# Making the lo parts of six output-projection weight tiles with adding transfers of GpSimd's queue

## The chip, the core and the metric

The kernel runs on one core of one Trainium2 chip. The metric is the device time of one execution in microseconds. The time before is 1053.56 us, the median of 3 runs (1052.34 to 1053.63).

## The reference

One decoder layer for 256 tokens of width 2048, all in float32:

```
h  = rmsnorm(x);  p = h @ w_in            # 16 heads: 8 dilated-window heads, 8 latent heads
A, B = the two attentions of p
x  = x + rmsnorm(concat(A, B) @ w_out)    # w_out: 2048 x 2048  <- the stage of the change
x  = x + rmsnorm(square(relu(rmsnorm(x) @ w_up)) @ w_down)
```

`concat(A, B)` is 256 x 2048 (`mixT`, transposed, in the kernel), so the output projection multiplies 2 blocks of 128 tokens by 16 blocks of 128 weight rows and 4 blocks of 512 weight columns.

## The kernel before

**Three products for one.** TensorE multiplies float32 in its faster form fp32r. To keep the accuracy, each operand is split in two: `hi` is the value rounded to fp32r, `lo` is what is left, `value - hi`. A product is then `hi*hi + lo*hi + hi*lo`, three matmuls that add up in one PSUM bank. The split of a weight tile takes two instructions (lines 293 and 294): ScalarE (ACT) writes `hi` as a rounded copy of the loaded tile `raw`, and VectorE (DVE) writes `lo = raw - hi`.

**Weight tiles.** All weights pass through the class `Weights` in one numbered series of tiles of 128 x 1024 (512 KB). `raw` has 5 buffers, `hi` and `lo` have 8 each. A tile is recorded (load, `hi`, `lo`) 7 tiles ahead of the one that TensorE works on. Loads are issued by SyncE (SP). A load waits until its `raw` buffer has been read for the last time; a split waits for its load and until TensorE has finished the tile that stood in the same `hi` and `lo` buffers, 8 tiles before.

**The output projection.** `ch_o` is four chunks of 512 columns, 0 to 3, each of 8 weight tiles; a tile holds two blocks of 128 rows. TensorE takes chunks 0 and 1 first, together; then chunk 2, tile by tile for both token blocks; then chunk 3, whose tiles 0 to 2 are taken for both token blocks at once and whose tiles 3 to 7 are taken for block 0 first and then for block 1. Tiles carry their number in the series: chunk 2 is tiles 105 to 112 and chunk 3 is tiles 113 to 120, so `hi106` is `hi` of the second tile of chunk 2. Tiles from 121 on are the first of `w_up`. A tile that both token blocks use at once is 12 matmuls.

**What else goes on there.** The last two heads of the latent attention (`b6`, `b7`) end inside chunks 0 and 1; their result `o_b` goes over ACT (`mixT_hi`) and DVE (`mixT_lo`) back to TensorE. When chunk 0 ends, `g_post` (1 MB, the gain of the norm) is loaded by SP into space that the attention has just left. ACT squares each finished chunk out of PSUM (`junko`) and DVE multiplies it by `g_post` (`yg`), which frees the PSUM bank. `powers()` squares `g_post` on ACT in four pieces (`junkg`), sums them on DVE (`gg`, `pws`, `t_pw`), and takes a power on GpSimd (`rstd_pw`), with which DVE scales `x`.

**Order.** Each engine runs its instructions in the order in which the program records them, and waits at the first one that is not ready. `Flow` records the attention and norm steps between the matmuls by an estimated clock of the author's; the weights are recorded by `Weights.emit` at the moment when TensorE's work reaches the tile 7 before.

Of the kernel before, what the change touches and what calls it, by code (L numbers as in the profile page):

```python
# [18 lines left out]
F32 = mybir.dt.float32  # L19
# [3 lines left out]
AF = mybir.ActivationFunctionType  # L23
OP = mybir.AluOpType
PSUM = bass.MemoryType.PSUM

P = 128
# [85 lines left out]
class Flow:  # L113
# [3 lines left out]
    def __init__(self):  # L117
        self.clock = 0.0
        self.chains = []
# [34 lines left out]
class Weights:  # L154


    def __init__(self, nc, pool, split, bufs, ahead):
        self.nc, self.pool, self.split_fn = nc, pool, split
        self.bufs, self.limit, self.ahead = bufs, bufs, ahead
        self.specs, self.tiles, self.done = [], [], []  # L160
        self.first, self.queue = {}, {}

    def plan(self, *spec):

# [13 lines left out]
    def emit(self, upto):  # L178
        upto = min(upto, self.done.index(False) + self.limit, len(self.specs))
        while len(self.tiles) < upto:  # L180
            i = len(self.tiles)
            spec = self.specs[i]
            make = len(spec) == 1
            if make or i not in self.queue:
                for f in self.first.pop(i, ()):
                    f()
            if not make:
                src, nk, n, g = (*spec, None)[:4]
                w = nk * n
                raw = self.load(src if len(src.shape) == 3 else src.rearrange("(k p) n -> p k n", p=P), w, f"raw{i}",  # L190
                                self.queue.get(i))
                for f in self.first.pop(i, ()):
                    f()
            hi = self.pool.tile([P, CW], F32R, tag="hi", bufs=self.bufs, name=f"hi{i}")
            lo = self.pool.tile([P, CW], F32R, tag="lo", bufs=self.bufs, name=f"lo{i}")
            if make:
                spec[0](hi, lo)
                self.tiles.append((hi, lo))
                continue

            def v(t):
                return t[:, :w].rearrange("p (k n) -> p k n", k=nk)

            cuts = [(o, min(o + 512, w)) for o in range(0, w, 512)] if i < FINE else [(0, w)]
            for o, e in cuts:
                self.split_fn(hi[:, o:e], lo[:, o:e], raw[:, o:e], g)
            self.tiles.append((v(hi), v(lo)))
# [43 lines left out]
def layer(nc, tc, io):  # L251
# [49 lines left out]
    def tok(t, k, b):  # L301
        return t[:, k, b * P:(b + 1) * P]

    weights = Weights(nc, wp, split, W_BUFS, W_AHEAD)
    gcol = con.tile([P, 8 + KD], F32, name="gcol")


# [17 lines left out]
    ch_o = [Chunk(weights, io["w_out"], n * 512, 512, K2, plan=False) for n in range(4)]  # L325
    for n, m in ((0, 6), (1, 6), (0, 2), (1, 2), (2, 8), (3, 8)):
        ch_o[n].plan(m)
    def up_weight(j, k):
        return io["w_up"][k * P:(k + 1) * P, j * CW:(j + 1) * CW]

# [32 lines left out]
    def seven_up(j, kp):  # L363
        def load():
            if j == FF // CW - 1 and kp:
                return [weights.load(up_weight(j, 2 * kp + i), CW, f"raw_w{j}_{kp}{i}") for i in range(2)]
            return load_two(late["ab"], nc.gpsimd if (j, kp) > (1, 0) else nc.sync,
                            io["w_up"][2 * kp * P:(2 * kp + 2) * P, j * CW:(j + 1) * CW])

        return seven(load, lambda: [late["up"].tile([P, CW], F32, tag="T", bufs=2, name=f"{n}{j}_{kp}") for n in "tu"])  # L370
# [21 lines left out]
    def plan_seven(sums, fs, after, more=(), last=()):  # L392

        at = max(len(weights.specs) - SUMS_AHEAD, after)
        for n, f in (*more, (0, sums), *((0, f) for f in last)):
            weights.first.setdefault(at - n, []).append(f)
        return [weights.plan(f) for f in fs], len(weights.specs)
# [4 lines left out]
    for j in range(FF // CW):  # L402
        wide_u.append([])
        for what, k in [("k", k) for k in range(KD)] if j == 0 else UP_STEPS:
            if what == "k":
                ts = [weights.plan(up_weight(j, k), 1, CW, gcol[:, 8 + k:9 + k])]
            else:
                ts, after = plan_seven(*seven_up(j, k), after)
            wide_u[j].append((what, k, ts))

    def down_weight(c, k):
        return io["w_down"][k * P:(k + 1) * P, c * CW:(c + 1) * CW]

    def seven_down(c, kp):
        def load():

            n = DOWN_SEVEN[c].index(kp)
            raw = dpl["ab"]
            if n % 2:
                raw = [uT[i].rearrange("p k s -> p (k s)") for i in range(2)] if c else late["c"]  # L420
            return load_two(raw, nc.gpsimd, io["w_down"][2 * kp * P:(2 * kp + 2) * P, c * CW:(c + 1) * CW])

        return seven(load, lambda: [late["st"][:, i * CW:(i + 1) * CW] for i in range(2)])

    dpl, left, skeep, wide_d = {}, {}, {}, []
    for c in range(2):
        wide_d.append([])
        for what, k in DOWN_STEPS[c]:
            if what == "k":
                ts = [weights.plan(down_weight(c, k), 1, CW)]  # L430
            else:
                q, parts_q, back = [lambda c=c, k=k, f=f: f(c, k) for f in (down_sums, down_split, down_back)]
                more = ((), (back,)) if c and k in SHARED else (((2, q), (1, parts_q)),)
                ts, after = plan_seven(*seven_down(c, k), after, *more)
# [218 lines left out]
    for half in range(2):  # L653
        qkv = {}
        for nms in (("qk", "v") if not half else "qkv"):
            accs = [acc for _, _, acc in proj(xT, [ch_a[half, nms]], f"{nms}{half}",
                                              bank_of=at_bank if (half, nms) == (0, "v") else None)]
            for i, nm in enumerate(nms):
                t = pa.tile([P, NB, 512], F32, tag=nm, name=f"{nm}_{half}")
# [215 lines left out]
    for ns in ((0, 1), (2,), (3,)):  # L875
# [4 lines left out]
        for c, b, acc in proj(mixT, [ch_o[n] for n in ns], f"o{ns[0]}", order, heads_done):  # L880
            n = ns[c]
            if not late:
# [8 lines left out]
                                  in_=io["norm_attn_post"].partition_broadcast(P).rearrange("p o d -> p (o d)"))  # L891
# [124 lines left out]
    for j in range(FF // CW):  # L1016
# [9 lines left out]
        for t, b in order:  # L1026
            what, k, tiles = steps[t]
# [172 lines left out]
    for g in (GT - 2, GT - 1):  # L1200
        if g == GT - 1:
            nc.gpsimd.drain()
        for b, n in PARTS:
            for kk in range(4):
                k = 4 * g + kk
# [40 lines left out]
def build(nc, arrays):  # L1246
    io = {n: nc.dram_tensor(f"in_{n}", a.shape, mybir.dt.from_np(a.dtype), kind="ExternalInput").ap()
          for n, a in arrays.items()}
    io["out"] = nc.dram_tensor("out_0", (S, D), F32, kind="ExternalOutput").ap()
    with tile.TileContext(nc) as tc, tc.manual_schedule():  # L1250
        layer(nc, tc, io)
# [12 lines left out]
```

## Time and profile before

| | |
|---|---|
| median of 3 runs | 1053.56 us (1052.34 to 1053.63) |
| the profiled execution's own time | 1052.05 us |
| its span, from the first to the last instruction | 1050.3 us |
| TensorE (PE) busy | 1039.0 us, 99% of the span |
| VectorE (DVE) busy | 811.0 us, 77% |
| ScalarE (ACT) busy | 625.4 us, 60% |
| GpSimd (POOL) busy | 61.5 us, 6% |
| granted TensorE clock | 0.998 |
| chunk 2 of the output projection, by TensorE | 309.7 to 331.5 us |
| chunk 3 | 331.5 to 354 us |

Between the span and the execution's own time lie 1.75 us outside the recorded instructions. The execution is 1.5 us below the median of the runs. In the tables of windows, `PE busy (x)` is the busy time and in brackets the number of instructions. In a timeline a row is: start, duration, engine, line, operation, output <- inputs, and in brackets the idle time before it with what ended it. Rows of DMA issues give the size of one transfer and the median time from issue to landing; POOLq and SPq are the queues of GpSimd and SyncE.

### The profile page before, as it was taken

What the parts mean: (1) busy time and instruction counts of PE and PEld (TensorE: products, weight loads), DVE (VectorE), ACT (ScalarE), POOL (GpSimd) and SP (SyncE); (2) the same over time, 40 slices, a digit from 0 to 9 for tenths busy, and PEclk for the clock granted to TensorE, in tenths of its full rate; (3) what the DMA queues carried; (4) which work ended last, traced back from release to release, by engine and by line L of the source; (5) the groups of instructions that cost most, each with busy time, mean ns of one, the idle gap of its engine ahead of it and who ended that gap; (6) DMA issues with size and microseconds to landing.
All of it is one profiled execution on the core that took longest, in us unless ns stands there. A gap on an engine that the chain in (4) does not pass through costs nothing.

```text
span 1050.3 us, 13459 instructions
## 1 busy us (share of the span) xinstructions
PE 1039.0 (99%) x4854; PEld 865.9 (82%) x4854; DVE 811.0 (77%) x1080; ACT 625.4 (60%) x834; POOL 61.5 (6%) x116
## 2 busy tenths in 40 slices
PE   9999999999999999999999999999999999999996
PEld 6888899888888788888888888888888888888885
DVE  6676536577557679879888798887899978989995
ACT  6675436565555467666665666666567564766661
POOL 0000000000000000010000000000000001112100
PEclk9999999999999999999999999999999999999999
DMA  8975447454447295646556465469788767788952
GB/s 298 371 230 155 140 127 239 141 166 155 141 170 234 77 344 174 224 143 238 194 189 201 145 234 194 151 227 319 246 276 315 267 223 259 268 300 313 381 186 81
DMA packets 80643, 229.34 MB, mean 218 GB/s; under 512 B 7616, under 2 KB 12224, under 8 KB 80192
## 3 DMA queue, kind: packets, MB, share of 16 engines
q1 hardware_dynamic: 65888, 176.45, 50.3%
q0 software_dynamic: 14112, 51.39, 14.2%
q8 instruction: 38, 0.62, 0.2%
q10 hardware_dynamic: 576, 0.64, 0.2%
q14 instruction: 29, 0.24, 0.1%
HBM read 212.72 MB, written 15.73 MB: 218 GB/s over the span
## 4 chain that ended last, share of the span: by engine, by line
PE 96%; DVE 1%; DMA 1%; issue 1%; ACT 0%; POOL 0%; DVEq 0%; POOLq 0%; ACTq 0%
PE y L283 26%; PE acc_u L283 26%; PE acc_o L283 8%; PE m L283 5%; PE md L283 5%; PE acc_v L283 4%; PE acc_qk L283 4%; PE acc_ckv L283 2%; PE acc_ukv L283 2%; PE acc_q L283 2%; PE acc_cq L283 2%; PE acc_k L283 2%; PE acc_uq L283 2%; PE rt L287 1%; PE sc_b L283 1%
## 5 line engine op out<-in xcount | busy, mean ns | idle before, releaser
L294 DVE TENSOR_TENSOR lo<-raw,hi 128x1024 fp32r<-128x1024 f32 (+3 forms) x213 | 241.7, 1152 | 91.5 <-ACT hi L293 90.7
L293 ACT ACTIVATE hi<-raw 128x1024 fp32r<-128x1024 f32 (+3 forms) x213 | 209.5, 999 | 77.6 <-PE y L283 20.8
L283 PE MATMUL acc_u<-hi,hT_hi 128*128 128x512 f32 x386 | 153.3, 397 | 0.0
L283 PE MATMUL acc_u<-hi,hT_lo 128*128 128x512 f32 x386 | 151.0, 391 | 0.4 <-DVE hT_lo L294 0.4
L283 PE MATMUL acc_u<-lo,hT_hi 128*128 128x512 f32 x386 | 150.7, 391 | 0.0
L283 PE MATMUL y<-hi,uhi 128*128 128x512 f32 x376 | 146.8, 390 | 0.0
L283 PE MATMUL y<-hi,ulo 128*128 128x512 f32 x376 | 146.5, 390 | 0.0
L283 PE MATMUL y<-lo,uhi 128*128 128x512 f32 x376 | 146.5, 390 | 0.0
L298 DVE SCALAR_TENSOR_TENSOR lo<-raw,gcol,hi 128x1024 fp32r<-128x1024 f32 x86 | 107.6, 1280 | 11.2 <-ACT hi L297 11.0
L297 ACT ACTIVATE hi<-raw,gcol 128x1024 fp32r<-128x1024 f32 x86 | 97.8, 1151 | 24.8 <-PE acc_u L283 10.9
L283 PEld LDWEIGHTS acc_u<-hi,hT_lo 128*128 128x128 f32 x386 | 72.5, 188 | 16.1 <-DVE hT_lo L294 0.8
L283 PEld LDWEIGHTS acc_u<-lo,hT_hi 128*128 128x128 f32 x386 | 72.6, 188 | 14.2
L283 PEld LDWEIGHTS acc_u<-hi,hT_hi 128*128 128x128 f32 x386 | 72.6, 188 | 13.9
L283 PEld LDWEIGHTS y<-hi,uhi 128*128 128x128 f32 x376 | 70.6, 188 | 14.6
L283 PEld LDWEIGHTS y<-hi,ulo 128*128 128x128 f32 x376 | 70.6, 188 | 14.6
L283 PEld LDWEIGHTS y<-lo,uhi 128*128 128x128 f32 x376 | 70.6, 188 | 14.5
L283 PE MATMUL acc_o<-hi,mixT_hi 128*128 128x512 f32 x128 | 51.9, 405 | 0.0
L294 DVE TENSOR_TENSOR lo<-st_down,hi 128x1024 fp32r<-128x1024 f32 x40 | 48.1, 1220 | 4.0 <-ACT hi L293 3.8
L283 PE MATMUL acc_o<-hi,mixT_lo 128*128 128x512 f32 x128 | 50.2, 392 | 0.0
L283 PE MATMUL acc_o<-lo,mixT_hi 128*128 128x512 f32 x128 | 50.0, 391 | 0.0
L293 ACT ACTIVATE hi<-ab 128x512 fp32r<-128x512 f32 (+1 forms) x38 | 32.0, 842 | 29.3 <-PE acc_u L283 24.4
L293 ACT ACTIVATE hi<-st_down 128x1024 fp32r<-128x1024 f32 x40 | 42.1, 1053 | 11.1 <-PE y L283 9.5
(322 smaller groups left out, 1986.3 us busy)
## 6 DMA issues: line engine op xcount, KB each, us to landing
raw<-in_w_down SPq DMA_DIRECT2D x88, 512.0 KB, 6.0
raw<-in_w_up SPq DMA_DIRECT2D x86, 512.0 KB, 4.5
raw<-in_w_in SPq DMA_DIRECT2D x55, 512.0 KB, 5.0
ab<-in_w_up POOLq DMA_DIRECT2D x36, 512.0 KB, 5.0
raw<-in_w_out SPq DMA_DIRECT2D x32, 512.0 KB, 4.3
ab_down<-in_w_down POOLq DMA_DIRECT2D x20, 512.0 KB, 6.4
ukeep<-ulo SPq DMA_DIRECT2D x15, 512.0 KB, 7.2
ulo<-ukeep POOLq DMA_DIRECT2D x15, 512.0 KB, 5.4
```

The costliest lines, as they stand in the source:

```text
L283: nc.tensor.matmul(out, a, b, start=start, stop=stop)
L287: nc.tensor.transpose(out, a, ident)
L293: nc.scalar.activation(hi, src, AF.Copy)
L294: nc.vector.tensor_tensor(out=lo, in0=src, in1=hi.bitcast(F32), op=OP.subtract)
L297: nc.scalar.activation(hi, src, AF.Copy, scale=g)
L298: nc.vector.scalar_tensor_tensor(out=lo, in0=src, scalar=g, in1=hi.bitcast(F32), op0=OP.mult, op1=OP.subtract)
```

## The change

For six tiles of the output projection `lo` is no longer written by VectorE. ScalarE writes `lo = -hi`, and a transfer issued by GpSimd, with an addition on the way, adds the float32 values to it.

- Tiles 106, 108, 110 and 112 (tiles 1, 3, 5, 7 of chunk 2; "sbuf"): SP loads `raw` as before. ACT writes `hi` (line 319 after the change) and then `lo = -hi` as a second rounded copy of `raw` with scale -1 (line 320). GpSimd issues the transfer `lo += raw` from SBUF to SBUF (line 321).
- Tiles 114 and 117 (tiles 1 and 4 of chunk 3; "hbm"): there is no `raw` and no load by SP. GpSimd loads the tile from HBM straight into `hi`, converted to fp32r on the way (line 315); ACT writes `lo = -hi` (line 316); GpSimd issues `lo += weights` from HBM (line 317), which reads the tile from HBM a second time.

```diff
--- before.py
+++ after.py
@@ -158,7 +158,7 @@
         self.nc, self.pool, self.split_fn = nc, pool, split
         self.bufs, self.limit, self.ahead = bufs, bufs, ahead
         self.specs, self.tiles, self.done = [], [], []
-        self.first, self.queue = {}, {}
+        self.first, self.queue, self.adds = {}, {}, {}
 
     def plan(self, *spec):
 
@@ -184,9 +184,11 @@
             if make or i not in self.queue:
                 for f in self.first.pop(i, ()):
                     f()
+            by = self.adds.get(i)
             if not make:
                 src, nk, n, g = (*spec, None)[:4]
                 w = nk * n
+            if not make and by != "hbm":
                 raw = self.load(src if len(src.shape) == 3 else src.rearrange("(k p) n -> p k n", p=P), w, f"raw{i}",
                                 self.queue.get(i))
                 for f in self.first.pop(i, ()):
@@ -201,6 +203,11 @@
             def v(t):
                 return t[:, :w].rearrange("p (k n) -> p k n", k=nk)
 
+            if by:
+                self.add_fn(hi, lo, src if by == "hbm" else raw, v)
+                self.tiles.append((v(hi), v(lo)))
+                continue
+
             cuts = [(o, min(o + 512, w)) for o in range(0, w, 512)] if i < FINE else [(0, w)]
             for o, e in cuts:
                 self.split_fn(hi[:, o:e], lo[:, o:e], raw[:, o:e], g)
@@ -301,7 +308,20 @@
     def tok(t, k, b):
         return t[:, k, b * P:(b + 1) * P]
 
+    def split_by_add(hi, lo, src, v):
+
+        if len(src.shape) == 2 and src.shape[0] != P:
+            src = src.rearrange("(k p) n -> p k n", p=P)
+            nc.gpsimd.dma_start(out=v(hi), in_=src)
+            nc.scalar.activation(lo, hi.bitcast(F32), AF.Copy, scale=-1.0)
+            nc.gpsimd.dma_start(out=v(lo), in_=src, accum_op=OP.add)
+        else:
+            nc.scalar.activation(hi, src, AF.Copy)
+            nc.scalar.activation(lo, src, AF.Copy, scale=-1.0)
+            nc.gpsimd.dma_start(out=lo.bitcast(F32), in_=src, accum_op=OP.add)
+
     weights = Weights(nc, wp, split, W_BUFS, W_AHEAD)
+    weights.add_fn = split_by_add
     gcol = con.tile([P, 8 + KD], F32, name="gcol")
 
 
@@ -325,6 +345,9 @@
     ch_o = [Chunk(weights, io["w_out"], n * 512, 512, K2, plan=False) for n in range(4)]
     for n, m in ((0, 6), (1, 6), (0, 2), (1, 2), (2, 8), (3, 8)):
         ch_o[n].plan(m)
+    for n, ts, how in ((2, (1, 3, 5, 7), "sbuf"), (3, (1, 4), "hbm")):
+        for t in ts:
+            weights.adds[ch_o[n].tiles[t][0]] = how
     def up_weight(j, k):
         return io["w_up"][k * P:(k + 1) * P, j * CW:(j + 1) * CW]
```

TensorE's order is the same before and after. On VectorE six subtractions are gone, in SyncE's queue the loads `raw114` and `raw117`; the rest keeps its order there. The two engines whose order changes are shown here; in the rows the numbers behind the underscore are buffer numbers.

GpSimd's instructions from the clearing of `krT` (attention) to the first `rstd_post` (the norm after the projection), before:

```order
L710 MEMSET krT_1891 128x512
L485 TENSOR_TENSOR rstd_pw_3002<-t_pw_3001,neg_half_82 128x2
L485 TENSOR_TENSOR rstd_post0_3196<-t_post0_3195,neg_half_82 128x1
L485 TENSOR_TENSOR rstd_post1_3312<-t_post1_3311,neg_half_82 128x1
L485 TENSOR_TENSOR rstd_pre20_3343<-t_pre20_3342,neg_half_82 128x1
```

The same stretch of GpSimd after the change:

```order
L733 MEMSET krT_1891 128x512
L321 DMA lo106_2779<-raw106_2776 128x1024
L321 DMA lo108_2836<-raw108_2833 128x1024
L321 DMA lo110_2898<-raw110_2895 128x1024
L321 DMA lo112_2945<-raw112_2942 128x1024
L315 DMA hi114_2983<-in_w_out 128x2x512
L317 DMA lo114_2984<-in_w_out 128x2x512
L508 TENSOR_TENSOR rstd_pw_3005<-t_pw_3004,neg_half_82 128x2
L315 DMA hi117_3052<-in_w_out 128x2x512
L317 DMA lo117_3053<-in_w_out 128x2x512
L508 TENSOR_TENSOR rstd_post0_3198<-t_post0_3197,neg_half_82 128x1
```

Eight transfers have come in. `rstd_pw` now stands behind six of them, and the load of `hi117` stands behind `rstd_pw`.

ScalarE's instructions from the end of chunks 0 and 1 (`junko`, out of their four PSUM banks) through the splits of chunk 2's last and chunk 3's first tiles, before:

```order
L293 ACTIVATE hi110_2895<-raw110_2893 128x1024
L802 ACTIVATE junko10_2905,ssy0_2433<-acc_o0_1_0_0_2448 128x512
L802 ACTIVATE junko11_2914,ssy1_2434<-acc_o0_1_1_0_2449 128x512
L293 ACTIVATE hi111_2921<-raw111_2919 128x1024
L816 ACTIVATE junkg0_2937,gg4_2437<-g_post_2859 128x512
L293 ACTIVATE hi112_2941<-raw112_2939 128x1024
L816 ACTIVATE junkg1_2954,gg4_2437<-g_post_2859 128x512
L293 ACTIVATE hi113_2961<-raw113_2959 128x1024
L816 ACTIVATE junkg2_2971,gg4_2437<-g_post_2859 128x512
L293 ACTIVATE hi114_2981<-raw114_2979 128x1024
L816 ACTIVATE junkg3_2988,gg4_2437<-g_post_2859 128x512
```

After, from the second copy of tile 112 to the split of tile 118:

```order
L320 ACTIVATE lo112_2945<-raw112_2942 128x1024
L839 ACTIVATE junkg1_2958,gg4_2437<-g_post_2861 128x512
L300 ACTIVATE hi113_2965<-raw113_2963 128x1024
L839 ACTIVATE junkg2_2975,gg4_2437<-g_post_2861 128x512
L316 ACTIVATE lo114_2984<-hi114_2983 128x1024
L839 ACTIVATE junkg3_2991,gg4_2437<-g_post_2861 128x512
L300 ACTIVATE hi115_3010<-raw115_3008 128x1024
L300 ACTIVATE hi116_3035<-raw116_3033 128x1024
L316 ACTIVATE lo117_3053<-hi117_3052 128x1024
L300 ACTIVATE hi118_3072<-raw118_3070 128x1024
```

The copies `lo112` (and, above these rows, `lo106`, `lo108` and `lo110`) are new on ScalarE. `lo114` and `lo117` stand where `hi114` and `hi117` stood, but read what GpSimd's transfers bring. The same kind of insertion stands between the last two steps of head b7: before it was the copy of `hi108` and then `mixT_hi` from `o_b7`, after it is

```order
L320 ACTIVATE lo108_2836<-raw108_2833 128x1024
L300 ACTIVATE mixT_hi_76<-o_b7_2840 128x256
```

with `hi108` ahead of both.

## The prediction

> **What bounds the kernel now.** I read the page's busy times first, then TensorE's waits, then the windows of 8 us over the stage that changes.
>
> ```profile
> span 1050.3 us, 13459 instructions
> PE 1039.0 (99%) x4854; PEld 865.9 (82%) x4854; DVE 811.0 (77%) x1080; ACT 625.4 (60%) x834; POOL 61.5 (6%) x116
> ...
> PE warm L505 <- DVE zero L502: 1.2, 1, 1.2
> PE acc_qk L283 <- ACT hi L293: 1.0, 2, 0.8
> PE acc_u L283 <- DVE hT_lo L294: 0.4, 1, 0.4
> PE qrt L287 <- DVE qT L744: 0.2, 1, 0.2
> ```
>
> TensorE is the bound: 1039.0 of 1050.3 us, and all its recorded waits together are 2.8 us, none of them for a weight tile of the output projection. So taking work off VectorE in this stage has almost nothing to give, and the change can only be felt if a tile that was ready in time comes late. What matters is by how much each of the six tiles was early, and how long its new way is.
>
> ```profile
> 302.00:310.00 8.00, 8.00 (x36) 6.37 (x36) 2.31 (x5) 2.71 (x6) 0.00 (x0) 1.00 0.92 314
> 310.00:318.00 8.00, 8.00 (x37) 6.64 (x36) 6.97 (x8) 7.97 (x16) 0.00 (x0) 1.00 0.97 343
> 318.00:326.00 8.00, 8.00 (x37) 6.64 (x36) 7.23 (x16) 3.40 (x5) 1.60 (x1) 1.00 0.91 281
> 326.00:334.00 8.00, 8.00 (x37) 6.60 (x36) 4.37 (x6) 4.01 (x7) 0.00 (x0) 1.00 0.53 178
> 334.00:342.00 8.00, 8.00 (x37) 6.64 (x36) 5.22 (x5) 3.78 (x4) 0.00 (x0) 1.00 0.71 231
> ```
>
> The columns are the stretch, its length, busy PE, PEld, DVE, ACT and POOL, the granted clock, the DMA share and GB/s. TensorE is never idle at full clock. What is scarce from 302 to 326 is the transfers (shares 0.92, 0.97, 0.91), because the loads held back behind `g_post` are being caught up, and from 310 to 318 ScalarE (7.97 of 8 us). The change adds to exactly these two.
>
> **When TensorE needs the tiles.** The first matmul of chunk 2 is at 309.72, the first that reads `lo114` at 334.42, the first that reads `lo117` at 341.22:
>
> ```profile
> 309.72 0.39 PE L283 MATMUL acc_o<-hi,mixT_hi 128*128 128x512 f32 x1
> ...
> 334.42 0.39 PE L283 MATMUL acc_o<-lo,mixT_hi 128*128 128x512 f32 x1
> ...
> 341.22 0.39 PE L283 MATMUL acc_o<-lo,mixT_hi 128*128 128x512 f32 x1
> ```
>
> They are found by counting rows of TensorE's order, which starts a matmul every 0.2267 us here ((341.22 - 309.72) / 139). By the same count `lo106` is due at 312.67, `lo108` at 318.1, `lo110` at 323.55 and `lo112` at 329.0.
>
> **The change, part by part.** *VectorE loses six subtractions.*
>
> ```profile
> L294 DVE TENSOR_TENSOR lo<-raw,hi 128x1024 fp32r<-128x1024 f32 x14 | 17.1, 1224 | 5.1 <-ACT hi L293 4.9
> ```
>
> That is 6 x 1.224 = 7.3 us of busy time off the path; no tile of the stage was waited for, so it is worth 0. *ScalarE gains four copies* (the "sbuf" tiles; the "hbm" tiles trade one for one), about 1.05 us each. One of them, `lo108`, stands ahead of head b7's `mixT_hi` (timelines of ScalarE, VectorE and TensorE):
>
> ```profile
> 299.86 1.05 ACT L293 ACTIVATE hi<-raw 128x1024 fp32r<-128x1024 f32 x1
> 301.46 0.39 ACT L293 ACTIVATE mixT_hi<-o_b 128x256 fp32r<-128x256 f32 x1 [0.54 <-PE o_b L283]
> ...
> 300.95 1.23 DVE L294 TENSOR_TENSOR lo<-raw,hi 128x1024 fp32r<-128x1024 f32 x1 [0.66 <-ACT hi L293]
> 302.09 0.42 DVE L294 TENSOR_TENSOR mixT_lo<-o_b,mixT_hi 128x256 fp32r<-128x256 f32 x1
> ...
> 302.56 0.50 PE L283 MATMUL acc_o<-hi,mixT_lo 128*128 128x512 f32 x1
> ```
>
> `hi108` ends at 300.91, `lo108` would end near 301.9, so `mixT_hi` starts 0.4 later than 301.46. `mixT_lo` was held to 302.09 by the subtraction of tile 108, which is gone, so it moves only to about 302.4. The matmul at 302.56 started right behind it; 0.3 us of TensorE are lost here, with nothing to hide them (bounds 0 and 0.5).
>
> *The transfers that add.* No row shows one. The nearest:
>
> ```profile
> ab<-in_w_up POOLq DMA_DIRECT2D x36, 512.0 KB, 5.0
> ukeep<-ulo SPq DMA_DIRECT2D x15, 512.0 KB, 7.2
> ulo<-ukeep POOLq DMA_DIRECT2D x15, 512.0 KB, 5.4
> c<-in_w_down POOLq DMA_DIRECT2D x8, 512.0 KB, 8.1
> ...
> L360 POOL DMA_DIRECT2D ab<-in_w_up x36 | 19.6, 544 | 251.3 <-DVE lo L294 223.7 <-DVE c L963 27.7
> ```
>
> At least an add is a plain transfer of GpSimd's queue into such a tile, 5.4 us. At most it is as long as reading the tile out and bringing it back one after the other, 7.2 + 5.4 = 12.6 us. It must fetch two operands for every value written, so I take the middle, 9.0 us; the nearest row is the 8.1. The plain load of `hi` by GpSimd, converting on the way, I take at 5.0 us (the `ab` row; bounds 5.0 and 8.1). Eight issues at 0.54 us are 4.3 us of GpSimd, which was idle.
>
> The Trainium skill ("Collectives: The Full Stack", Part 3, "The bandwidth ceiling") says that an adding transfer costs not by its arithmetic but by its two source reads, and moves at about half the rate of a copy (32.35 against 62.28 GB/s). No row here shows it; it speaks for a price above 5.4.
>
> *The chain of the last tile.* The rows of the timelines of ScalarE, VectorE and GpSimd that it starts from:
>
> ```profile
> 308.39 1.06 ACT L293 ACTIVATE hi<-raw 128x1024 fp32r<-128x1024 f32 x1 [3.17 <-DMA raw<-in_w_out]
> 309.73 1.06 ACT L293 ACTIVATE hi<-raw 128x1024 fp32r<-128x1024 f32 x1 [0.27 <-DMA raw<-in_w_out]
> 310.70 0.57 ACT L802 ACTIVATE junko<-acc_o 128x512 bf16<-128x512 f32 x1
> ...
> 314.49 0.62 ACT L816 ACTIVATE junkg<-g_post 128x512 bf16<-128x512 f32 x1
> ...
> 316.67 1.05 ACT L293 ACTIVATE hi<-raw 128x1024 fp32r<-128x1024 f32 x1
> 317.62 0.62 ACT L816 ACTIVATE junkg<-g_post 128x512 bf16<-128x512 f32 x1
> ...
> 319.34 0.17 DVE L484 TENSOR_SCALAR t_pw<-pws 128x2 f32<-128x2 f32 x1
> ...
> 319.59 1.60 POOL L485 TENSOR_TENSOR rstd_pw<-t_pw,neg_half 128x2 f32<-128x2 f32 x1 [112.66 <-DVE t_pw L484]
> ```
>
> ScalarE waited for the load of tile 109 until 308.39. The add of tile 108, issued near 301.9, now shares the engines with that load. Its 0.52 MB read twice are 1.05 MB; at the 314 GB/s of that window 3.3 us; half of it ahead of tile 109's bytes delays ScalarE by 1.7 us (bounds 0 and 3.3). Then ScalarE runs without a gap as before, with two copies of 0.97 us more (the step from 309.73 to 310.70): `lo112` ends at 314.49 + 1.7 + 2 x 0.97 = 318.1. GpSimd issues the add of 112 there and at 318.7 the load of `hi114` (its buffer, that of tile 106, was left by TensorE near 315). It lands after 5.0 us, and 1.7 us later still for the add just ahead of it in the same queue: 325.4 (bounds 323.7 and 327.2). ScalarE, which stands at `lo114` from 316.67 + 1.7 + 1.94 = 320.3, waits 5.1 us. `lo114` ends at 326.4, its add lands at 335.4; TensorE asks at 334.42 + 0.3 = 334.7 and waits 0.7.
>
> Behind `lo114` is the fourth `junkg`: 0.7 us, then about 0.6 us of `gg`, `pws` and `t_pw` on a VectorE with time: 327.7. `rstd_pw` takes 1.60: 329.3. Only now does GpSimd issue `hi117`; it lands at 334.3, `lo117` is written by 335.35, its add lands 9.0 us later at 344.35. TensorE, late by 0.3, asks at 341.5. So it waits 2.85 us, which includes the 0.7. Sum: 0.3 + 2.85 = 3.1 us.
>
> Rows for what stands around the new steps: VectorE's first product with `g_post`, the issue of `g_post`, SP's loads of the stage, and the first use of the scaled `x`.
>
> ```profile
> L803 DVE TENSOR_TENSOR yg<-acc_o,g_post 128x512 f32<-128x512 f32 x6 | 4.0, 687 | 6.5 <-DMA g_post<-in_norm_attn_post 3.9 <-ACT junko L802 2.5
> ...
> 301.58 0.34 SPq L890 DMA_DIRECT2D g_post<-in_norm_attn_post  x1
> ...
> 306.44 1.29 DVE L803 TENSOR_TENSOR yg<-acc_o,g_post 128x512 f32<-128x512 f32 x2 [3.93 <-DMA g_post<-in_norm_attn_post]
> ...
> raw<-in_w_out SPq DMA_DIRECT2D x12, 512.0 KB, 5.8
> ...
> 349.14 2.08 DVE L841 SCALAR_TENSOR_TENSOR x<-yg,rstd_post,x 128x512 f32<-128x512 f32 x3 [0.66 <-POOL rstd_post L485]
> ```
>
> *What queues behind.* Behind ScalarE's wait for `hi117` stand `hi118` (due 342.4, ready with its subtraction near 337.6), the two `junko` of chunk 2 (their banks are next needed by `acc_u` near 354) and tiles 119 and 120, due 1.4 us apart after 343.7: late by some 6 us against before, still ahead of use. SP's loads 113, 116 and 119 now wait for the adds of 108, 110 and 112, which held their `raw` buffers; 116 is issued near 322 and needed by ScalarE near 328, so with the 5.8 us of landing that SP's loads take in this stage it just fits. `rstd_pw` moves from 319.59 to about 327.7; the scaled `x` that waits for it is first used at 349.14.
>
> **Against which time.** The profiled execution took 1052.05 us (span 1050.3 and 1.75 around it); with 3.1 it becomes 1055.2. The median of the runs was 1053.56, so I forecast 1053.56 + 3.1 = 1056.7 us.
>
> **Rivals.** *Everything stays hidden* (not slower). The case turns on the add's duration: the add of `lo117` starts at 335.35 and is due at 341.5, so up to 6.15 us it costs nothing, and a plain 5.4 is under that. For it: the lower row, and the windows of 326 to 342 with DMA shares of 0.53 and 0.71, where a transfer meets little. Against it: two operands per value. Then only b7's 0.3 us remain: 1053.9. The Trainium skill ("DMA: Bandwidth & Descriptors", "Anatomy of one DMA") gives 2.0 us fixed and bytes at 436 GB/s; with doubled reads that is an estimate of 4.4 us for an add on an empty queue, and the sum by it is this rival's.
>
> *The add of 108 holds up `g_post`* (slower, early). `g_post` landed just before 306.44, `yg` freed chunk 2's first bank at 307.1, TensorE asked at 309.72: 2.6 us of room, 2.9 with b7's 0.3. The add's 3.3 us, all ahead of `g_post`, would cost 0.4; if it takes twice that, 3.7. With b7: 4.0, 1057.6. Against it: the transfers share, and `g_post` is issued at 301.58, 0.3 us and more ahead of it.
>
> *Adds far slower than 12.6 us*, at 20 say: `lo117` would land 11 us after 344.35, total 14, 1067.7. Nothing shows such a rate; a small chance.
>
> *Faster.* VectorE's spare time would have to shorten a wait of TensorE. Behind this stage only the 0.4 us for `hT_lo` is one, and the b7 step could win at most another 0.3: 1052.9 at best, which a measurement here cannot tell from no change (about 0.2%, 2.1 us). Only something that no row shows could do more.
>
> *The change does not do what it says*: if the converting load did not round `hi`, `lo` would be 0 and only accuracy would suffer; the time is the same.
>
> **How the numbers follow.** The last adds late by between 1.8 and about 8 us: 0.50. Hidden: 0.33. `g_post` held up: 0.08. Far slower: 0.05. Faster: 0.04. That is 0.63 slower, 0.33 same, 0.04 faster. The range starts under the hidden case less half the spread of the runs, 1052.8. At the top, an add of 12.6 instead of 9.0 gives 3.6 more, ScalarE's delay of 3.3 instead of 1.7 gives 1.6 more: 3.1 + 5.2 = 8.3, 1062. The likeliest case alone reaches from 1055.6 to 1062.
>
> **What would show it.** In the changed profile TensorE's waits should have a row on a transfer into `lo`, largest at tile 117, and chunk 3's end should lie about 3 us later; ScalarE's `lo<-hi` should wait some 5 us twice; `rstd_pw` should start near 327. The transfers' landing times decide: 9 is my case, 6.1 and less the rival. I am wrong if TensorE shows no wait in chunk 3, or if the first wait is at 309.72.

## The result and the profile after

The kernel is slower: 1062.37 us (median of 4 runs, 1061.74 to 1064.05) against 1052.95 us (4 runs, 1051.72 to 1053.63) beside it, a ratio of 1.0093 with a 95% interval of 1.0076 to 1.0111. That is 9.4 us more where 3.1 were forecast, and just above the range's end of 1062.0. The profiled execution took 1061.8 us.

The page after, its busy times:

```profile
span 1060.0 us, 13465 instructions
PE 1042.6 (98%) x4854; PEld 868.5 (82%) x4854; DVE 803.7 (76%) x1074; ACT 628.2 (59%) x838; POOL 67.3 (6%) x124
```

VectorE did lose its 7.3 us of work (811.0 to 803.7), and nobody was waiting for it. TensorE's waits (us in total, times, longest):

```profile
PE acc_o L290 <- DMA lo<-in_w_out: 7.0, 2, 4.5
```

This row is new: two waits for the adding transfers from HBM, 7.0 us in all. The windows, with the columns as before, show where:

```profile
318.00:326.00 8.00, 8.00 (x37) 6.62 (x36) 2.61 (x3) 5.07 (x10) 1.64 (x2) 1.00 1.04 242
326.00:334.00 8.00, 8.00 (x37) 6.64 (x36) 0.00 (x0) 1.64 (x4) 0.29 (x1) 1.00 0.83 250
334.00:342.00 8.00, 3.49 (x13) 2.57 (x12) 5.67 (x14) 1.93 (x3) 2.37 (x3) 0.90 0.83 198
342.00:350.00 8.00, 6.80 (x26) 5.14 (x25) 4.44 (x6) 6.45 (x10) 1.21 (x1) 0.89 0.56 124
```

From 318 to 334 TensorE is busy without a gap, and the transfers' share from 318 to 326 is 1.04, where before it was 0.91. Then TensorE stands still, and its granted clock falls to 0.90 and 0.89. Its timeline there, rows around the two waits:

```profile
335.24 0.39 PE L290 MATMUL acc_o<-hi,mixT_hi 128*128 128x512 f32 x1
340.14 0.52 PE L290 MATMUL acc_o<-lo,mixT_hi 128*128 128x512 f32 x1 [4.51 <-DMA lo<-in_w_out]
340.45 0.63 PE L290 MATMUL acc_o<-hi,mixT_lo 128*128 128x512 f32 x1
340.88 0.63 PE L290 MATMUL acc_o<-hi,mixT_hi 128*128 128x512 f32 x1
...
343.86 0.40 PE L290 MATMUL acc_o<-lo,mixT_hi 128*128 128x512 f32 x1
...
348.41 0.39 PE L290 MATMUL acc_o<-hi,mixT_hi 128*128 128x512 f32 x1
351.30 0.47 PE L290 MATMUL acc_o<-lo,mixT_hi 128*128 128x512 f32 x1 [2.50 <-DMA lo<-in_w_out]
```

The first wait is for `lo114`, the second for `lo117`. In steps from one start to the next, at 0.227 us each in normal work, the sum is 4.90 - 0.23 = 4.67 lost at `lo114`, 0.08 on the step behind it, 8 steps that took 3.41 instead of 1.81 us (1.60 lost, at half clock), and 2.89 - 0.23 = 2.66 at `lo117`: 9.0 us. This sum is only another way of saying when `lo117` landed. TensorE reaches tile 117 early in any case, so the half clock between the two waits costs nothing here: without it the second wait would be 1.6 longer (whether that longer wait would have slowed the clock behind it is open).

What made `lo117` land so late is in the chain of waits from 315 us on (start, duration, what):

```profile
319.85 1.05 ACT lo L320
...
321.19 0.51 POOL lo L321
...
321.74 10.52 DMA hi<-in_w_out
...
332.36 1.07 ACT lo L316
...
333.71 1.21 POOL lo L317
334.92 0.53 POOL rstd_pw L508
335.45 7.97 DMA hi<-in_w_out
...
343.52 1.07 ACT lo L316
...
344.88 6.28 DMA lo<-in_w_out
...
351.30 10.26 PE acc_o L290 x44
```

Read downward it is one tile's work after the other: `lo112` on ScalarE, the add of 112 issued, the load of `hi114` (10.52 us), `lo114`, the add of 114 issued, `rstd_pw`, the load of `hi117` (7.97 us), `lo117`, its add (6.28 us), TensorE. The two loads are 18.5 us of it. They were forecast at 6.7 and 5.0.

Why a load of 512 KB takes 8 us can be read in the transfers. The next rows are GpSimd's queue in one-microsecond windows from 335 on, five in a row, then that of 341 to 342 with SP's queue ahead of it (packets, MB, share of the 16 engines):

```profile
q0 software_dynamic: 16, 0.03, 32.9%
q0 software_dynamic: 45, 0.09, 85.4%
q0 software_dynamic: 99, 0.20, 111.8%
q0 software_dynamic: 108, 0.21, 108.3%
q0 software_dynamic: 89, 0.16, 62.3%
...
q1 hardware_dynamic: 63, 0.21, 56.5%
q0 software_dynamic: 98, 0.18, 55.3%
```

The add of 114 was issued at 333.71 and the load of `hi117` at 335.45. By 339 the queue has moved 0.03 + 0.09 + 0.20 + 0.21 = 0.53 MB, which is one tile (0.52 MB), and the add lands at 340.0. From 339 to 343 it moves 0.51 MB more, and the load lands at 343.4. So the load's bytes begin when those of the add are through, 3.5 us after its issue, where the add's own began within 2; and then they take 4 us, because SP's loads have half of the engines. One link earlier it is the same: the bytes of `hi114`, issued at 321.74, begin when the add of 112 has moved its 0.52 MB, near 327.

### The profile page after: what moved, and what is told of

Same layout as the page of the kernel before. It is cut to its first block, busy times and chain, and to the rows that moved or that the text cites. A ratio compares the mean times of both kernels' runs of the same rounds, so it can differ in the third digit from the quotient of the medians.

```text
span 1060.0 us, 13465 instructions
## 1 busy us (share of the span) xinstructions
PE 1042.6 (98%) x4854; PEld 868.5 (82%) x4854; DVE 803.7 (76%) x1074; ACT 628.2 (59%) x838; POOL 67.3 (6%) x124
## 4 chain that ended last, share of the span: by engine, by line
PE 92%; DMA 4%; DVE 1%; issue 1%; ACT 1%; POOL 0%; SPq 0%; DVEq 0%; POOLq 0%; ACTq 0%
PE y L290 25%; PE acc_u L290 25%; PE m L290 5%; PE md L290 5%; PE acc_qk L290 4%; PE acc_o L290 4%; PE acc_v L290 4%; PE acc_ckv L290 2%; PE acc_ukv L290 2%; PE acc_q L290 2%; PE acc_cq L290 2%; PE acc_k L290 2%; DMA hi<-in_w_out 2%; PE acc_uq L290 2%; PE rt L294 1%
## 5 line engine op out<-in xcount | busy, mean ns | idle before, releaser
L301 DVE TENSOR_TENSOR lo<-raw,hi 128x1024 fp32r<-128x1024 f32 (+3 forms) x207 | 234.2, 1149 | 99.2 <-ACT hi L300 98.8
L300 ACT ACTIVATE hi<-raw 128x1024 fp32r<-128x1024 f32 (+3 forms) x207 | 203.0, 997 | 73.7 <-PE y L290 20.3
```

Source lines behind the costliest of these rows:

```text
L300: nc.scalar.activation(hi, src, AF.Copy)
L301: nc.vector.tensor_tensor(out=lo, in0=src, in1=hi.bitcast(F32), op=OP.subtract)
```

## The experiments

Each experiment was timed against the kernel before, and the loss is the difference of the two medians. The code of the edits is shortened; the remarks behind `#` in it belong to this document.

**Each half of the change alone.** The first keeps only the four adds from SBUF, the second only the two tiles from HBM.

```diff
-    for n, ts, how in ((2, (1, 3, 5, 7), "sbuf"), (3, (1, 4), "hbm")):
+    for n, ts, how in ((2, (1, 3, 5, 7), "sbuf"),):        # first
+    for n, ts, how in ((3, (1, 4), "hbm"),):               # second
```

> Only tiles 106, 108, 110 and 112 get their lo by an adding transfer; 114 and 117 are split as before. Theory A (the time is lost in GpSimd's two converting loads of hi114 and hi117, one after the other in its queue and ahead of their adds): no wait of TensorE in chunks 2 and 3, kernel before plus 0.1 to 0.5 us. Rival B (the four adds of chunk 2 fill the transfer engines and delay everything behind them): at least half of the 9.4 us stays, 4 us or more. The adds themselves should land 5 to 10 us after their issue.

> Only tiles 114 and 117 are made by GpSimd's transfers; 106 to 112 are split as before. Theory A: hi114 is issued near 315 with no add ahead of it, lands 6 to 9 us later, its add is in time; hi117 is issued near 326 to 329 behind rstd_pw, lands 8 us later, so its add lands near 341 to 345 against 341.2: 0 to 5 us over the kernel before, with a wait at tile 117 only. Rival B (the adds of chunk 2 are the cause): no wait at all, loads landing in 5 us, the time of the kernel before.

The first took 1052.6 us against 1052.88, ratio 0.9997 (0.9987 to 1.0006), the second 1052.21 us, 0.9994 (0.9985 to 1.0004). Each half is free, so the loss comes from the two together. The second one's GpSimd timeline and TensorE's wait show by how little:

```profile
316.88 0.87 POOL L315 DMA_DIRECT2D hi<-in_w_out  x1 [108.67 <-PE acc_o L290]
326.22 1.24 POOL L317 DMA_DIRECT2D lo<-in_w_out  x1 [8.46 <-ACT lo L316]
...
327.95 2.01 POOL L315 DMA_DIRECT2D hi<-in_w_out  x1
336.60 1.21 POOL L317 DMA_DIRECT2D lo<-in_w_out  x1 [6.63 <-ACT lo L316]
```

```profile
PE acc_o L290 <- DMA lo<-in_w_out: 0.4, 1, 0.4
```

The last add is issued at 336.60, lands 6.3 later, and TensorE waits 0.4: the chain of two tiles alone fits with nothing to spare. Against it (the two clocks agree to some 0.3 us) the changed kernel issues the load of `hi114` 4.9 later (321.74), lands it in 10.5 instead of 7.9, and that of `hi117` in 8.0 instead of 7.2. Together 8.3 us, and its last add is issued 8.3 later (344.88). The first of these comes from the load's place behind the add of 112, which waits for `lo112` on ScalarE; the second goes with that add's bytes ahead of it. For the third, 0.8 us, no run singles out a cause.

**Without the conversion, and without GpSimd's loads.** In the first, GpSimd loads tiles 114 and 117 plainly into `raw`, and they are then split like the "sbuf" tiles. In the second SP loads them.

```diff
-    for n, ts, how in ((2, (1, 3, 5, 7), "sbuf"), (3, (1, 4), "hbm")):
+    for n, ts, how in ((2, (1, 3, 5, 7), "sbuf"), (3, (1, 4), "sbuf")):   # both
+            if n == 3:                                                     # first only
+                weights.queue[ch_o[n].tiles[t][0]] = nc.gpsimd
```

> As the changed kernel, but tiles 114 and 117 are loaded by GpSimd plainly into raw (float32, no conversion), ScalarE writes hi and lo from it (one copy more each), and the add reads raw. The issues stand where they stood in GpSimd's queue. If the conversion is what makes the loads take 10.5 and 8.0 us: they land in 5 to 6, and the loss over the kernel before falls from 9.4 to 2 to 4 us. If the place in the queue behind an add and the shared engines are the cause: the loads take 8 to 10.5 still, and with the copies the loss is 10 to 12 us.

> All six tiles with raw loaded by SP and an add from raw; no load by GpSimd is left. Theory A: six adds are hidden, before plus 0.1 to 0.8 us, no wait of TensorE on tiles 114 and 117. Rival B, and the recorded prediction's own view that an add takes 9 us and is itself the price: a wait at 114 or 117 of 1 us or more.

With GpSimd's plain loads it took 1061.29 us against 1052.88, 1.008 (1.0065 to 1.0095), and with SP's loads 1053.75 us, 1.0014 (1.0002 to 1.0025). The plain loads landed in 8.8 and 7.0 us where the converting ones took 10.5 and 8.0, so the conversion is at most 1.0 to 1.7 us of a load. The adds were shorter too (4.6 and 4.9), but each tile now needs two copies on ScalarE (1.06 us each) instead of one, and the loss stays nearly whole, 8.4 us. That is between the two sums that were expected, 2 to 4 and 10 to 12, which had not counted the shorter adds. The step from the first to the second moves the same bytes in another queue, and 7.5 us are gone. The trace with SP's loads has no wait of TensorE for a `lo`, though its last two adds took 8.3 and 8.7 us. But that execution is the fastest of ten (1051.80 to 1058.09), and what the slower ones waited for is open. GpSimd's timeline with its plain loads is the same chain once more (the add at 332.89 follows ScalarE's second copy of tile 114, which ends at 332.60, whatever the bracket names):

```profile
321.73 0.93 POOL L175 DMA_DIRECT2D raw<-in_w_out  x1
332.89 0.88 POOL L321 DMA_DIRECT2D lo<-raw  x1 [10.23 <-PE acc_o L290]
...
334.63 0.77 POOL L175 DMA_DIRECT2D raw<-in_w_out  x1
344.03 0.88 POOL L321 DMA_DIRECT2D lo<-raw  x1 [8.63 <-ACT lo L320]
```

**The same transfers, the loads earlier.** Tiles 114 and 117 get `hi` buffers of their own, and both loads are issued right behind the add of 110, ahead of that of 112; the buffers are there so that the loads needn't wait for others to come free.

```diff
-            nc.gpsimd.dma_start(out=v(hi), in_=src)
+            # issued when tile 111 is recorded, behind the add of 110:
+                    hi = late["po"].tile([P, CW], F32R, name=f"hx{i}")
+                    nc.gpsimd.dma_start(out=hi.rearrange("p (k n) -> p k n", k=nk), in_=s.rearrange("(k p) n -> p k n", p=P))
```

> As the changed kernel, with the same transfers, but hi114 and hi117 have buffers of their own, so that their two loads are issued together right behind the add of tile 110 and ahead of the add of 112, wait for no buffer, and neither waits for the other's lo. Theory C (the loss is the chain in GpSimd's queue: add of 112, load of 114, add of 114, rstd_pw, load of 117, add of 117, each waiting for the one before): the loads are issued near 317 and 318 and land near 326 to 328, both adds are in time, before plus 0 to 1 us. Rival D (the eight transfers are simply too much for the engines in this stage): the loss stays above 4 us.

1053.11 us against 1053.2, 1.0002 (0.9993 to 1.0012): the whole loss is gone, with the same transfers. GpSimd's timeline and TensorE's wait for `lo`:

```profile
315.38 1.79 POOL L357 DMA_DIRECT2D hx<-in_w_out  x2
...
324.07 1.22 POOL L317 DMA_DIRECT2D lo<-in_w_out  x1 [3.59 <-ACT lo L316]
...
330.60 1.45 POOL L317 DMA_DIRECT2D lo<-in_w_out  x1 [4.58 <-ACT lo L316]
```

```profile
PE acc_o L290 <- DMA lo<-raw: 0.2, 1, 0.2
```

The loads landed in 7.2 and 9.3 us and the HBM adds in 9.7 and 10.3, longer than the 6.3 of the changed kernel, and still nothing is late, because the last add is issued at 330.60 instead of 344.88. So it isn't the amount of traffic, nor how long an add takes, but the place of the two loads in GpSimd's queue. The buffers of their own don't explain it: in the changed kernel neither load waited for one, each was issued as soon as the instruction ahead let it (321.19 to 321.74 behind the add of 112, 334.79 to 335.45 behind `rstd_pw`).

**Fewer adds ahead of the chain.** The first leaves tile 112 to VectorE, the second tile 108.

```diff
-    for n, ts, how in ((2, (1, 3, 5, 7), "sbuf"), (3, (1, 4), "hbm")):
+    for n, ts, how in ((2, (1, 3, 5), "sbuf"), (3, (1, 4), "hbm")):       # first
+    for n, ts, how in ((2, (1, 5, 7), "sbuf"), (3, (1, 4), "hbm")):       # second
```

> As the changed kernel without the add of tile 112, the one just ahead of the load of hi114. Theory C: hi114 is issued near 317 instead of 321.7, the whole chain moves 4 to 5 us ahead; no wait at tile 114, one of 2 to 4.5 us at tile 117; before plus 2 to 6 us. Rival D: one transfer of eight less, before plus 7 to 9 us.

> As the changed kernel without the add of tile 108, the one that ran beside the loads after g_post (10.4 us). Theory C: the loads of 109 to 113 land 2 to 3 us sooner, ScalarE reaches lo112 and GpSimd hi114 that much sooner, the chain moves by 2.5 to 3.5 us: before plus 4 to 7 us. If the early adds do not matter: before plus 9 us.

Without 112: 1055.84 us against 1053.2, 1.0027 (1.0018 to 1.0037). Without 108: 1060.6 us, 1.0068 (1.0053 to 1.0083). The one add that stands straight ahead of the load of `hi114` is worth 6.8 of the 9.4 us (9.4 less the 2.6 left), that of 108, two adds earlier, 2.0 (the loss of 7.4 is a little over the 4 to 7 expected). Without 112 the load is issued at 317.08, and lands in 8.0. It stands behind an add here too, that of 110, issued at 316.53, and lands as soon as with none ahead (7.9). So the add of 112 costs in two ways: its wait for `lo112` holds the issue of the load up by 4.7 us (321.74 against 317.08), and behind its bytes, beside SP's loads, the load takes 2.5 us longer to land. What is left is one wait, at `lo117`:

```profile
345.25 0.47 PE L290 MATMUL acc_o<-lo,mixT_hi 128*128 128x512 f32 x1 [2.80 <-DMA lo<-in_w_out]
```

Here the load of `hi117` took 9.3 us, 2.1 more than with the two tiles alone, where the same wait was 0.4.

**The same transfers as copies.** All six bring the value itself instead of adding it.

```diff
-            nc.gpsimd.dma_start(out=v(lo), in_=src, accum_op=OP.add)
+            nc.gpsimd.dma_start(out=v(lo), in_=src)
-            nc.gpsimd.dma_start(out=lo.bitcast(F32), in_=src, accum_op=OP.add)
+            nc.gpsimd.dma_start(out=lo.bitcast(F32), in_=src)
```

> As the changed kernel, but the six transfers into lo copy instead of adding (the addition is left out, so lo holds the whole value). Tells what the addition itself costs. If an add costs two reads where the copy costs one: landings at least 1.2 us shorter each, the loss falls by 2 to 4 us. If the addition is free and the transfers cost by their place and the traffic: landings within 0.5 us of before, loss 8 to 9.5 us.

1057.94 us against 1053.2, 1.0041 (1.0026 to 1.0056): half of the loss is left without any addition. The loss fell by 4.7, more than the 2 to 4 expected, although the landings didn't each become 1.2 us shorter: that of tile 112 went from 7.8 to 7.7 only, those from HBM from 6.3 to 4.2. The first transfer into `lo`, which meets nothing else, shows the price of adding by itself. GpSimd's queue from 296 to 297 us and the landing time, in the adding kernel:

```profile
q0 software_dynamic: 48, 0.20, 102.3%
lo<-raw POOLq DMA_DIRECT2D x1, 512.0 KB, 4.7
```

And in the copying one:

```profile
q0 software_dynamic: 99, 0.37, 91.9%
lo<-raw POOLq DMA_DIRECT2D x1, 512.0 KB, 3.1
```

An add fills the engines at 0.20 MB/us, a copy at 0.37, and the add lands 1.6 us later. The Trainium skill ("Collectives: The Full Stack", Part 3, "The bandwidth ceiling") has the adding phase of a collective, a ring over several cores, at about half the rate of the copying one, because the add needs two source reads. The 0.20 against 0.37 here, within one core, is near that ratio; the reads themselves no run here shows.

**One link at a time.** As in the experiment with early loads, but for tile 114 alone, and then for tile 117 alone.

```diff
-            if how == "hbm":            # both tiles early
+            if how == "hbm" and t == 1: # first: only tile 114
+            if how == "hbm" and t == 4: # second: only tile 117
```

> Only tile 114 has a buffer of hi of its own, with its load issued right behind the add of 110 and ahead of that of 112; hi117 stays where it was, behind the add of 114 and rstd_pw. If the loss is made by two loads in series that each stand behind an add in GpSimd's queue, taking out the first link brings the second 7 us forward or more: hi117 is issued near 326, lands 7 to 9.5 us later because the add of 114 goes first, and lo117 lands near 344 where TensorE asks near 342: loss 0 to 2.5 us, no wait at tile 114, no drop of the clock. If the second load alone made the loss, 2.5 us or more stay with the same 8.0 us of landing and the same late rstd_pw; if the amount of traffic did, the time stays near 1062.

> Only tile 117 has a buffer of hi of its own, loaded right behind the add of 110; hi114 stays behind the add of 112. By the same theory the first link stays whole and is 0 to 3 us longer, because one more load now goes ahead of the add of 112 in the queue: TensorE waits 4.5 to 7.5 us at tile 114, its clock drops for some 3.4 us (1.6 us), and nothing at tile 117: loss 6 to 9 us. If the second link were the main one, the loss would be under 3 us.

With `hi114` early: 1057.3 us against 1052.8, 1.0043 (1.0028 to 1.0058), a loss of 4.5 where 0 to 2.5 was expected, so the second link was underrated again. Its load, issued at 327.39, stands behind the adds of 112 and 114, which landed in 8.2 and 9.2 us, and itself takes 10.5; there is one wait, of 3.2 us, at `lo117`, in the profiled execution without a drop of the clock. With `hi117` early: 1059.73 us, 1.0069 (1.0052 to 1.0086), a loss of 6.9, inside the expected 6 to 9. Here the wait is at `lo114`, and the rest is the clock:

```profile
340.27 0.76 PE L291 MATMUL acc_o<-lo,mixT_hi 128*128 128x512 f32 x1 [4.70 <-DMA lo<-in_w_out]
340.83 0.63 PE L291 MATMUL acc_o<-hi,mixT_lo 128*128 128x512 f32 x1
...
345.52 0.54 PE L291 MATMUL acc_o<-lo,mixT_hi 128*128 128x512 f32 x1
345.90 0.40 PE L291 MATMUL acc_o<-hi,mixT_lo 128*128 128x512 f32 x1
```

Either link alone makes TensorE late, and of the kernels with all eight transfers only the one with both loads moved ahead has no loss. None of the ten kernels beats the kernel before by more than a measurement can tell.

## Why the prediction was wrong

**Right.** The sign, the place and the chain. TensorE was the bound, work taken off VectorE was worth nothing, and the chain of the last tile, with ScalarE's two waits for `hi` and `rstd_pw` between them, decided. The deadlines by counting rows held: the changed trace runs 0.94 us behind that of before from the start (the row at 294.43 below against 295.37), and TensorE asked for `lo114` at 335.47, that is 334.53 by the clock of before, forecast 334.7.

**The step of b7** was 0.1 us instead of 0.3. A matmul ahead of the stretch and one behind it, before:

```profile
294.43 0.49 PE L287 MATMUL pT_b<-ident,s_b 128*128 128x128 f32 x3
302.90 0.40 PE L283 MATMUL acc_o<-hi,mixT_hi 128*128 128x512 f32 x1
```

and after:

```profile
295.37 0.49 PE L294 MATMUL pT_b<-ident,s_b 128*128 128x128 f32 x3
303.93 0.40 PE L290 MATMUL acc_o<-hi,mixT_hi 128*128 128x512 f32 x1
```

303.93 - 302.90 is 1.03, and 0.94 of it was there already. It also came about in another way than forecast: TensorE was held at the matmul that reads `mixT_hi` (303.12, 0.47 us behind the one ahead of it), and the short hold of before at the one that reads `mixT_lo` (302.56) is gone.

**The term that failed is the load of `hi`.** Forecast and measured, by the clock of before:

| step | forecast | measured |
|---|---|---|
| `lo112` written | 318.1 | 320.0 |
| load of `hi114` issued, its length | 318.7, 6.7 | 320.8, 10.5 |
| add of 114 issued, its length | 326.4, 9.0 | 332.8, 6.3 |
| load of `hi117` issued, its length | 329.3, 5.0 | 334.5, 8.0 |
| add of 117 issued, landed | 335.35, 344.35 | 343.9, 350.2 |
| TensorE late at `lo117` | 2.85 | 9.0 |

The two loads were 3.8 and 3.0 us longer than forecast. `lo112` came 1.9 us later, since ScalarE waited not only for the load of tile 109 (until 311.86, 310.9 by the clock of before; forecast 310.1) but 1.2 us for the next one as well:

```profile
311.86 1.06 ACT L300 ACTIVATE hi<-raw 128x1024 fp32r<-128x1024 f32 x1 [5.60 <-DMA raw<-in_w_out]
314.14 1.06 ACT L319 ACTIVATE hi<-raw 128x1024 fp32r<-128x1024 f32 x1 [1.22 <-DMA raw<-in_w_out]
```

From the issue of the add of 114 to that of `hi117`'s load it took 1.7 us instead of 2.9, since `rstd_pw` held the queue for 0.66 and not 1.60, and the last add took 6.3 instead of 9.0. The rest is three hand-overs between engines, forecast 0.2 to 0.45 too short each, 1.1 in all. So `lo117` lands 1.9 + 3.8 + 3.0 + 1.1 - 1.2 - 2.7 = 5.9 us later than forecast, and TensorE, which asked 0.15 earlier than thought and starts 0.14 after the landing, is late by 9.0 instead of 2.85. The price of an add, on which the forecast put its whole doubt, was set too high; the loss is larger all the same.

The step itself failed in two ways. The 5.0 us came from the transfers into `ab`, in another stretch; here each load was issued behind an add whose bytes went first, and shared the engines with SP's loads: even with the two tiles alone they took 7.9 (here with no add ahead) and 7.2. The forecast had seen that for `hi114`, with 1.7 us, and not for `hi117`, although by its own numbers the add of 114 was under way from 326.4 to 335.4 when `hi117` was issued at 329.3. And the range left a bound out: 5.0 to 8.1 was written for the load, but the top of the range took only the add's 12.6 and ScalarE's 3.3. With 8.1 for both loads it would have reached 6.2 us higher and held the result. Two smaller slips change nothing here: the bound of 327.2 for `hi114` is 327.0 by its own terms, and half the spread of the three runs is 0.65 us, with which the range starts at 1053.2 and not at 1052.8.

**The signs.** A new wait on transfers into `lo` and a later `rstd_pw` came, but not in their sizes. The larger wait is at tile 114 (4.5 us, forecast 0.7), not at 117; ScalarE waited 9.3 and 7.6 us for `hi` instead of some 5 twice; `rstd_pw` started at 333.85 by the clock of before instead of near 327. All three go with the longer loads.

**The rivals.** That everything stays hidden is true of each half of the change and not of the whole; its condition, an add of at most 6.15 us, looked at the one duration that didn't decide. The add of 108 did land late, 10.4 us after its issue, beside `g_post`, but the first matmuls of chunk 2 waited for nothing. Adds far slower than 12.6 did not occur: 4.7 to 10.4 in the changed kernel. The estimate of 4.4 us for an add on an empty queue, worked out from the Trainium skill's "DMA: Bandwidth & Descriptors" ("Anatomy of one DMA"), was close for the first add (4.7), and said nothing of what the load behind it waits.

## What to carry to other kernels

A transfer has two prices, the time until it lands and the time for which it holds up what is issued behind it on the same queue, the issuing engine's own wait for its input included; a chain that goes load, compute, transfer, load through one queue pays the second at every link. Before handing work to a queue that looks idle, write down the order of its issues and ask of each what stands ahead of it and what that one waits for; here moving two issues ahead of the last three adds, for two more buffers of `hi`, was worth all 9.4 us. And an upper bound that is written down beside a term belongs in the range, once for each time that the term is used.

## What the runs showed of the hardware

**The clock after an idle stretch.** After idle stretches of TensorE of 3.5, 4.3, 4.5, 4.7 and 4.7 us its matmuls started every 0.427 us instead of 0.227, for 8, 9, 8, 5 and 11 of them (copies, plain loads, the changed kernel, without 108, `hi117` early); after 2.5, 2.8 and 3.2 us they didn't. The bound need not be sharp: the kernel with 3.2 us (`hi114` early) had a mean granted clock of 0.998 in its profiled execution and of 0.996 in the other three, which took 0.7 to 1.0 us more. Where such a drop follows the last wait it is lost on top of it: in the kernel with copies one wait of 3.5 us and 8 x 0.2 = 1.6 us make 5.1, and the time was 4.7 over. The Trainium skill ("TensorE: Matmul & The Clock Gate", Part 1, "What's actually happening") has half the clock after an idle window of about 3.4 us, and the full one after another such window of work, the windows running free of the kernel; both the bound between 3.2 and 3.5 us in the traces and the uneven number of slow matmuls agree.

**Issues.** In the changed kernel an adding issue is recorded with 0.86 to 1.05 us from SBUF and 1.21 from HBM, a converting load with 0.91 and 1.09. With copies in place of the adds it is 0.54 to 0.73, and the plain loads of the same tiles took 0.77 and 0.93; so an addition makes the issue longer, and for a conversion that is not shown. The next instruction starts earlier than the record ends: 0.55 us after an add from SBUF (321.19 to 321.74), 1.08 after one from HBM (333.71 to 334.79).
